# Order of VectorE's split-offs, place of a transpose step, two weight forms and a drain in a two-layer decoder trunk

## The chip, the cores and the metric

The kernel runs on 1 core of one Trainium2 chip. The metric is the device time of one execution in microseconds; 3 executions are shown for the kernel before. The engines are TensorE (PE in the profile; PEld is its weight load), VectorE (DVE), ScalarE (ACT), GpSimd (POOL) and SyncE (SP), each with its own in-order queue of instructions; transfers are issued from SP's and POOL's queues.

## The reference

Two decoder layers on one sequence of 256 tokens with 1024 features, all in float32. Each layer adds to h an attention (16 heads of 64), a gated feed-forward part of width 2816 and a gated input embedding. Layer 0's attention has a learned forget gate added to the logits, layer 1's a relative-position bias; with 256 tokens there is a single block of keys, so both are plain causal attentions with a bias.

```python
for i in range(DEPTH):
    u = _rmsnorm(h, attn_norm_g[i])
    ...
    h = h + _merge_heads(o) @ fox_w_o[j]
    ...
    u = _rmsnorm(h, ffn_norm_g[i])
    gu = u @ ffn_w_in[i]
    h = h + (jax.nn.silu(gu[..., :D_FF]) * gu[..., D_FF:]) @ ffn_w_out[i]
    gate = jax.nn.sigmoid(_rmsnorm(h, ple_norm_g[i]) @ ple_w_gate[i])
    h = h + gate * (p[i] @ ple_w_up[i])
return _rmsnorm(h, final_norm_g)
```

## The kernel before

**Three matmuls for one.** Each float32 operand is split into a high half (rounded to fp32r) and a low half (what is left), and `mm3` makes high by high, high by low and low by high.

**The weights' path.** All weights are one stream of 512 KB tiles in the order of use. SP loads tile i into `raw` (6 buffers; line 153, for the gapped form line 178, for the entry form line 138). ScalarE copies it to `whi` (line 157), VectorE subtracts to get `wlo` (line 158); both have 6 buffers. So the load of raw i + 6 is issued when wlo i is made, and whi i + 6 waits until PE has used whi i. Each matmul triple reads whi twice and wlo once, and the third matmul of a step in the program's order is the first that needs wlo. The triples of two or four heads or tiles may be interleaved.

**Forms.** `blocks()` gives eight blocks of 128 columns side by side; with ENTRY the first two blocks' wlo lie 8 columns further on and the rest 64 (two subtractions, of 256 and 768 columns, line 142). `gapped()` leaves a gap behind the first block in whi and wlo alike (1080 columns, line 180); the host packs its weights with that gap.

**Attention.** `_plan` gives the steps of a layer: `qk` j is `project(j)`, which makes pair j's q and k (pq, 48 matmuls out of two weights) and calls `scale()`: VectorE multiplies by the norm's row (qkt, line 453), ScalarE makes qkh (line 273) and VectorE qkl (line 274). `scores` of two pairs runs the matmuls sp out of qkt, qkh and qkl, then VectorE adds the bias (e, eight instructions, line 484), ScalarE takes the exponential with a sum (line 488), VectorE the reciprocal (rc, line 497). For pairs 0 to 5 ScalarE applies it (line 506), VectorE transposes (et, line 512) and GpSimd sends it through DRAM and loads it back (back). For pairs 6 and 7 VectorE applies it itself (line 501), and the step `turn` transposes on PE (pp, line 531), with ScalarE evicting into pt (line 534). `values` of two pairs makes po out of back or pt and v, and splits it into o's high half (ScalarE, line 273) and low half (VectorE, line 274). `wo` (hf, c) multiplies o of pairs 2c and 2c + 1 by one weight tile, 24 matmuls into two banks. The banks of wo (four) stay open over the layer; the other steps turn over the rest of the eight banks.

**What sets the order.** The tile framework's scheduler orders each engine's instructions by the order in the code and by priorities; `tc.issue_after(x)` adds an edge from x to what is made inside. Weights are made well ahead of their use, as buffers allow.

The plan's part around the change, and the split before it:

```python
("values", 0, 1), ("scores", 4, 5), ("wo", 0, 0), *pairs(6),
("values", 2, 3), ("scores", 6, 7), ("wo", 1, 0), ("wo", 0, 1), ("wo", 1, 1),
("values", 4, 5), ("turn", 6, 7), ("wo", 0, 2), ("values", 6, 7), ("wo", 1, 2)]
```

Of the kernel before, what the change touches and what calls it, by code (L numbers as in the profile page):

```python
# [30 lines left out]
ALU = mybir.AluOpType  # L31
# [43 lines left out]
def trunk(ctx: ExitStack, tc: tile.TileContext, xh, xg, wx, xr, pt, w, cst, gf, rel, hot, rvm, out):  # L75
# [10 lines left out]
    def f32(ap):  # L86
        return ap.bitcast(F32)
# [37 lines left out]
    hr = hw[:, 2].rearrange("p (k s) -> p k s", s=S)  # L125
    hx = [gx[:, GX - S:], hw[:, 0, 0:S], hw[:, 1, 0:S]] + [hr[:, k] for k in range(KT - 3)]

    def half(at=0, entry=0):


        i = state["next"]
        state["next"] += 1
        if i not in (1, 2):
            raw = work.tile([P, HW + LINE], F32, tag="raw", bufs=RAW, name=f"raw{i}")
        ht, lt = (work.tile([P, HW + 2 * LINE], F32R, tag=n, bufs=6, name=f"{n}{i}") for n in ("whi", "wlo"))
        hi, lo = ht[:, at:at + HW], lt[:, at:at + HW]
        if entry:
            state["sp"] = nc.sync.dma_start(raw[:, 0:HW], w[i - 2][:, 0:HW])
            nc.scalar.activation(hi, raw[:, 0:HW], AF.Copy)  # L139
            ats = [(at + FURTHER, 0, entry), (at + LINE, entry, HW)]  # L140
            for a, c0, c1 in ats:
                nc.vector.tensor_tensor(lt[:, a + c0:a + c1], raw[:, c0:c1], f32(hi[:, c0:c1]), op=ALU.subtract)  # L142
            return hi, [lt[:, a + k * P:a + (k + 1) * P] for a, c0, c1 in ats for k in range(c0 // P, c1 // P)]
        if i in (1, 2):
            raw = hw[:, i - 1, S:]
        parts = 2 if i < 2 else 1
        for q in range(parts):
            c = slice(q * HW // parts, (q + 1) * HW // parts)
            if i in (1, 2):
                at = slice(c.start + (S if q else 0), c.stop + S)  # L150
                nc.sync.dma_start(hw[:, i - 1, at], wx[i - 1][:, at])
            else:
                state["sp"] = nc.sync.dma_start(raw[:, c], w[max(i - 2, 0)][:, c])
            if i + q == 0:
                nc.vector.tensor_copy(hi[:, c], raw[:, c])
            else:
                nc.scalar.activation(hi[:, c], raw[:, c], AF.Copy)  # L157
            nc.vector.tensor_tensor(lo[:, c], raw[:, c], f32(hi[:, c]), op=ALU.subtract)  # L158
        return hi, lo

    def later(to, src):
# [9 lines left out]
    def gapped(first=0):  # L171

        i = state["next"]
        state["next"] += 1
        raw = work.tile([P, HW + LINE], F32, tag="raw", bufs=RAW, name=f"raw{i}")
        at = slice(APART + FURTHER, APART + FURTHER + WW)
        ht, lt = (work.tile([P, HW + 2 * LINE], F32R, tag=n, bufs=6, name=f"{n}{i}")[:, at] for n in ("whi", "wlo"))
        state["sp"] = nc.sync.dma_start(raw[:, 0:WW], w[i - 2])
        nc.scalar.activation(ht, raw[:, 0:WW], AF.Copy)
        nc.vector.tensor_tensor(lt, raw[:, 0:WW], f32(ht), op=ALU.subtract)  # L180
        cs = [bool(n) * GAP + n * P for n in (_entered(first).index(k) for k in range(KT))]
        return [[t[:, c:c + P] for c in cs] for t in (ht, lt)]

# [87 lines left out]

    def split(hi, lo, src):
        nc.scalar.activation(hi, src, AF.Copy)  # L273
        nc.vector.tensor_tensor(lo, src, f32(hi), op=ALU.subtract)

    def tokens(o, x, t, w, start, stop):

# [115 lines left out]
    def attention(layer, nm, mid, early, nf):  # L393
# [26 lines left out]

        o = work.tile([P, NP, 2, S], F32R, tag="act", name=f"o{layer}")
        oh, ol = o[:, :, 0], o[:, :, 1]
        qk, pq, sm, pts = {}, {}, {}, {}
        bias = add = None

        def project(j):

            bk = bank(f"pq{layer}_{j}")
            for a in range(2):
                if layer and j == 2 and a == 0:  # L430
                    hi, lo = gapped()
                else:
                    hi, lo = blocks(ENTRY if j == 0 and a == 0 else ())
                for k in range(KT):
                    last = mm3(bk[:, a * S:(a + 1) * S], (hi[k], lo[k]), nm.k(k),
                               start=(k == 0), stop=(k == KT - 1))
                if (j, a) == (layer, 0):
                    with tc.issue_after(last.ins), tc.high_priority():
                        nm.spread(-0.125)
                        scale()  # L440
                if layer and j == 0 and a == 0:
                    with tc.issue_after(last.ins):
                        nm.root()
            pq[j] = bk
            if (j, layer) != (0, 1):
                scale()

        def scale():

            for j in sorted(pq):  # L450
                bk = pq.pop(j)
                t = work.tile([P, 2, S], F32, tag="qkt", bufs=2, name=f"qkt{layer}_{j}")
                nc.vector.tensor_tensor(t.rearrange("p a s -> p (a s)"), bk,
                                        nm.row.rearrange("p a s -> p (a s)"), op=ALU.mult)

                th = work.tile([P, 3 * P], F32R, tag="qkh", bufs=2, name=f"qkh{layer}_{j}")
                tl = work.tile([P, 3 * P], F32R, tag="qkl", bufs=2, name=f"qkl{layer}_{j}")
                split(th, tl, t.rearrange("p a s -> p (a s)")[:, P:])
                qk[j] = t, th, tl

        def scores(*js):

            rows = [slice(s * DH, (s + 1) * DH) for s in range(2)]
            heads = [(2 * j + s, d, qk[j], bank(f"sp{layer}_{2 * j + s}")) for j in js for s, d in enumerate(rows)]
            for _, d, (t, _, _), sp in heads:
                mm(sp[:, 0:P], t[d, 0, 0:P], t[d, 1, 0:P], start=True, stop=add is None, skip_group_check=True)
            for n, (q, k) in enumerate(((1, 1), (1, 2), (2, 1))):
                for _, d, t, sp in heads:
                    got = mm(sp[:, P:3 * P], t[q][d, 0:P], t[k][d, P:], start=False, stop=(n == 2 and add is None),
                             skip_group_check=True)  # L470
            if add:
                for i, _, _, sp in heads:
                    got = add(i, sp)
            sl = (slice(0, P), slice(P, 3 * P))
            es = []
            for n, j in enumerate(js):
                del qk[j]
                e = work.tile([P, 2, 3 * P], F32, tag="e", bufs=4, name=f"e{layer}_{j}")
                mn = tiny.tile([P, 2, 2, 2], F32, tag="mn", bufs=4, name=f"mn{layer}_{j}")
                es.append((j, e, mn))  # L480
                for s in range(2):
                    i, _, _, sp = heads[2 * n + s]
                    for q, b in enumerate(bias(i)):
                        last = nc.vector.tensor_tensor_reduce(e[:, s, sl[q]], sp[:, sl[q]], b, 1.0, 3.0e38,
                                                              ALU.add, ALU.min, mn[:, 0, s, q:q + 1])
                for s in range(2):
                    for q in range(2):
                        nc.scalar.activation(e[:, s, sl[q]], e[:, s, sl[q]], AF.Exp, scale=-1.0,  # L488
                                             bias=mn[:, 0, s, q:q + 1], accum_out=mn[:, 1, s, q:q + 1])
            with tc.issue_after(last.ins):  # L490
                for j, e, mn in es:
                    finish(j, e, mn, sl)
# [262 lines left out]
    def ple(nm, ut):  # L755
# [19 lines left out]
        for c in range(4):  # L775
            pair_unit(bks[0], c, half(), nm.k)
            if c == 1:
                nm.root()
                table(AF.Sigmoid, nm.col[:, 0:1])
            if c == 2:  # L780
                for hf in range(2):
                    for t in range(2):
                        turn(t, hf)
# [85 lines left out]
def _plan(layer):  # L869

    def pairs(j):
        return [("qk", j), ("qk", j + 1)]

    first = ([("row", k) for k in range(4)] + [("gate",)] if layer == 0 else
             [("v", 0, 0), ("v", 0, 1), ("v", 1, 0), ("v", 1, 1), ("root",)])
    return [*first, ("qk", 0), ("bias",), ("qk", 1),
            ("v", 0, 2), ("v", 0, 3), ("scores", 0, 1), *pairs(2),
            ("v", 1, 2), ("scores", 2, 3), ("v", 1, 3), *pairs(4),
            ("values", 0, 1), ("scores", 4, 5), ("wo", 0, 0), *pairs(6),
            ("values", 2, 3), ("scores", 6, 7), ("wo", 1, 0), ("wo", 0, 1), ("wo", 1, 1),  # L880
            ("values", 4, 5), ("turn", 6, 7), ("wo", 0, 2), ("values", 6, 7), ("wo", 1, 2)]


def _entered(first):
# [130 lines left out]
```

## Time and profile before

| what | value |
|---|---|
| median of 3 executions | 652.67 us (651.58 to 658.07) |
| profiled execution, its own time | 652.5 us |
| its span | 650.7 us |
| mean granted TensorE clock | 0.996 |
| matmuls on PE | 5320, busy 638.6 us |
| VectorE, ScalarE, GpSimd busy | 449.6, 381.8, 46.8 us |

The span runs from the first to the last instruction, and the profiled execution's own time is 1.8 us longer. A row of the timeline gives the start, the busy time, the engine, the line, the operation with the tile written and those read, the count, and in brackets the idle time before it with what ended it. The windows view gives for a stretch its length, PE's busy time with the count of matmuls, the granted clock, the share of the DMA engines and GB/s. A waits row reads: who waited, for whom, us in total, times, longest.

### The profile page before, as it was taken

How to read it: one execution, taken by the hardware profiler on the slowest of the kernel's cores; microseconds unless marked ns; L12 is line 12 of the kernel's file. 1: busy time of each engine (PE TensorE's matmuls, PEld its weight loads, DVE VectorE, ACT ScalarE, POOL GpSimd, SP SyncE). 2: the span in 40 equal slices, each digit the busy share in tenths (PEclk: the TensorE clock that was granted, in tenths of full speed). 3: DMA queues.
4: the chain of work that ended last, by engine and by line, in shares of the span. 5: the costliest groups of instructions: out<-in, count | busy, mean ns of one | idle time of the engine just before them, and what ended most of it. 6: DMA issues, size and time to landing. Idle time of an engine off the chain costs nothing.

```text
span 650.7 us, 13215 instructions
## 1 busy us (share of the span) xinstructions
PE 638.6 (98%) x5320; PEld 614.9 (94%) x5320; DVE 449.6 (69%) x730; ACT 381.8 (59%) x662; POOL 46.8 (7%) x81
## 2 busy tenths in 40 slices
PE   9999999999999999999999999999999999999994
PEld 7998998999999999999989999899999999999984
DVE  6877794786666666658696877578666666666764
ACT  7788764664444444456766887657444444444762
POOL 1003330100000000000000333000000000000001
PEclk9999999999999999999999999999999999999998
DMA  8859884397676666666467688635766666666401
GB/s 337 301 182 311 255 261 134 103 316 235 193 234 207 232 201 210 194 191 195 162 241 278 203 264 264 179 121 182 234 190 193 194 191 194 195 212 192 159 1 66
DMA packets 39582, 133.51 MB, mean 205 GB/s; under 512 B 4896, under 2 KB 8032, under 8 KB 39520
## 3 DMA queue, kind: packets, MB, share of 16 engines
q1 hardware_dynamic: 35840, 122.81, 59.2%
q0 software_dynamic: 3264, 9.44, 4.6%
q8 instruction: 42, 0.69, 0.4%
q10 hardware_dynamic: 416, 0.40, 0.2%
q14 instruction: 20, 0.16, 0.1%
HBM read 126.84 MB, written 8.94 MB: 209 GB/s over the span
## 4 chain that ended last, share of the span: by engine, by line
PE 86%; ACT 5%; issue 4%; DVE 4%; DMA 1%; POOL 0%; POOLq 0%; ACTq 0%
PE gu L92 37%; PE fo L92 18%; PE pq L92 9%; PE wo L92 7%; PE v L92 5%; PE pg L92 5%; DVE wlo L158 2%; PE pu L92 2%; ACT e L488 2%; ACT whi L157 1%; PE po L92 1%; ACT e L506 1%; PE sp L92 1%; DMA gx<-xg 1%; ACT v L419 1%
## 5 line engine op out<-in xcount | busy, mean ns | idle before, releaser
L158 DVE TENSOR_TENSOR wlo<-raw,whi 128x1024 fp32r<-128x1024 f32 (+1 forms) x192 | 232.3, 1217 | 101.6 <-ACT whi L157 101.2
L157 ACT ACTIVATE whi<-raw 128x1024 fp32r<-128x1024 f32 (+1 forms) x191 | 199.1, 1054 | 139.9 <-issue 55.9
L92 PE MATMUL gu<-g,whi 128*128 128x256 f32 x1408 | 241.9, 277 | 0.0
L92 PEld LDWEIGHTS gu<-g,whi 128*128 128x128 f32 x1408 | 212.4, 188 | 0.0
L92 PE MATMUL gu<-g,wlo 128*128 128x256 f32 x704 | 194.7, 277 | 0.0
L92 PEld LDWEIGHTS gu<-g,wlo 128*128 128x128 f32 x704 | 132.2, 188 | 0.0
L92 PE MATMUL fo<-fp,whi 128*128 128x256 f32 x704 | 121.1, 276 | 0.0
L92 PEld LDWEIGHTS fo<-fp,whi 128*128 128x128 f32 x704 | 106.3, 188 | 0.1
L92 PE MATMUL fo<-fp,wlo 128*128 128x256 f32 x352 | 97.3, 276 | 0.0
L92 PE MATMUL pq<-g,whi 128*128 128x256 f32 x512 | 90.0, 280 | 0.0
L92 PEld LDWEIGHTS pq<-g,whi 128*128 128x128 f32 x512 | 78.3, 189 | 0.6 <-issue 0.2
L92 PE MATMUL pq<-g,wlo 128*128 128x256 f32 x256 | 71.4, 279 | 0.0
L92 PEld LDWEIGHTS fo<-fp,wlo 128*128 128x128 f32 x352 | 66.1, 188 | 0.0
L92 PEld LDWEIGHTS pq<-g,wlo 128*128 128x128 f32 x256 | 48.1, 188 | 0.0
L273 ACT ACTIVATE fp<-sg 128x256 fp32r<-128x256 f32 x44 | 18.2, 417 | 49.3 <-DVE sg L657 49.3
L92 PE MATMUL wo<-o,whi 128*128 128x256 f32 x256 | 45.5, 281 | 0.0
L229 POOL TENSOR_TENSOR col<-ms,nhalf 128x2 f32<-128x2 f32 x6 | 9.4, 1564 | 473.7 <-DVE ms L227 473.7
L142 DVE TENSOR_TENSOR wlo<-raw,whi 128x256 fp32r<-128x256 f32 (+1 forms) x40 | 26.0, 688 | 24.2 <-ACT whi L139 24.2
L92 PE MATMUL v<-whi,g 128*128 128x512 f32 x128 | 40.8, 394 | 0.4 <-ACT g L195 0.4
L92 PEld LDWEIGHTS wo<-o,whi 128*128 128x128 f32 x256 | 38.7, 188 | 1.1 <-issue 0.6
L653 DVE TENSOR_TENSOR gut<-gu,row 128x512 f32<-128x512 f32 x44 | 30.0, 690 | 10.4 <-PE gu L92 10.3
L139 ACT ACTIVATE whi<-raw 128x1024 fp32r<-128x1024 f32 x20 | 21.2, 1062 | 26.7 <-PE gu L92 24.0
(159 smaller groups left out, 771.1 us busy)
## 6 DMA issues: line engine op xcount, KB each, us to landing
raw<-w SPq DMA_DIRECT2D x210, 512.0 KB, 4.2
d<-et POOLq DMA_DIRECT2D x12, 384.0 KB, 3.5
back<-d POOLq DMA_DIRECT2D x48, 96.0 KB, 6.9
d<-d SPq DMA_DIRECT2D x4, 768.0 KB, 5.6
bias<-d SPq DMA_DIRECT2D x4, 512.0 KB, 6.4
raw<-w SPq DMA_DIRECT2D x3, 540.0 KB, 3.5
h<-xh SPq DMA_DIRECT2D x4, 256.0 KB, 7.3
hw<-wx SPq DMA_DIRECT2D x1, 640.0 KB, 6.4
```

What stands on the lines that cost most here:

```text
L92: state["pe"] = nc.tensor.matmul(*a, **k)
L139: nc.scalar.activation(hi, raw[:, 0:HW], AF.Copy)
L142: nc.vector.tensor_tensor(lt[:, a + c0:a + c1], raw[:, c0:c1], f32(hi[:, c0:c1]), op=ALU.subtract)
L157: nc.scalar.activation(hi[:, c], raw[:, c], AF.Copy)
L158: nc.vector.tensor_tensor(lo[:, c], raw[:, c], f32(hi[:, c]), op=ALU.subtract)
L229: nc.gpsimd.tensor_tensor(self.col, ms, nhalf, op=ALU.pow)
L273: nc.scalar.activation(hi, src, AF.Copy)
L419: nc.scalar.activation(v[:, t, hf * HC:(hf + 1) * HC], bks[t], AF.Copy, scale=nm.col[:, t:t + 1])
L488: nc.scalar.activation(e[:, s, sl[q]], e[:, s, sl[q]], AF.Exp, scale=-1.0, bias=mn[:, 0, s, q:q + 1], accum_out=mn[:, 1, s, q:q + 1])
L506: nc.scalar.activation(e[:, s, sl[q]], e[:, s, sl[q]], AF.Copy, scale=rc[:, s, q:q + 1])
L653: nc.vector.tensor_tensor(t.rearrange("p a s -> p (a s)"), bks[f], nm.row.rearrange("p a s -> p (a s)"), op=ALU.mult)
```

## The change

It has four parts.

- A new function `behind` makes an instruction with an edge from `state["dv"]`. `scores` sets that to the low half (qkl) of its last pair. Every wlo made after the first `scores` goes through `behind`, so it may not be issued ahead of that qkl.
- In the plan `("turn", 6, 7)` stands ahead of `("values", 4, 5)`.
- The first half of qk 4 has the entry form in both layers, and layer 1's first half of qk 2 is no longer gapped; the host's packing follows.
- GpSimd drains behind the call of the last norm's `root`.

```diff
+    def behind(make):
+
+        if "dv" not in state:
+            return make()
+        with tc.issue_after(state["dv"].ins):
+            return make()
...
-                nc.vector.tensor_tensor(lt[:, a + c0:a + c1], raw[:, c0:c1], f32(hi[:, c0:c1]), op=ALU.subtract)
+                behind(lambda: nc.vector.tensor_tensor(lt[:, a + c0:a + c1], raw[:, c0:c1], f32(hi[:, c0:c1]),
+                                                       op=ALU.subtract))
...
-            nc.vector.tensor_tensor(lo[:, c], raw[:, c], f32(hi[:, c]), op=ALU.subtract)
+            behind(lambda: nc.vector.tensor_tensor(lo[:, c], raw[:, c], f32(hi[:, c]), op=ALU.subtract))
...
-        nc.vector.tensor_tensor(lo, src, f32(hi), op=ALU.subtract)
+        return nc.vector.tensor_tensor(lo, src, f32(hi), op=ALU.subtract)
...
-                if layer and j == 2 and a == 0:
-                    hi, lo = gapped()
-                else:
-                    hi, lo = blocks(ENTRY if j == 0 and a == 0 else ())
+                hi, lo = blocks(ENTRY if j in (0, 4) and a == 0 else ())
...
-                split(th, tl, t.rearrange("p a s -> p (a s)")[:, P:])
+                low[j] = split(th, tl, t.rearrange("p a s -> p (a s)")[:, P:])
...
+            state["dv"] = low[js[-1]]
...
                 nm.root()
+                nc.gpsimd.drain()
...
-            ("values", 4, 5), ("turn", 6, 7), ("wo", 0, 2), ("values", 6, 7), ("wo", 1, 2)]
+            ("turn", 6, 7), ("values", 4, 5), ("wo", 0, 2), ("values", 6, 7), ("wo", 1, 2)]
```

What that does to the queues, in layer 1. In the names below the number behind a weight's whi or wlo is its place in the stream (133, 134 and 135 belong to the three wo steps behind `scores` 6, 7, and 136 to wo (0, 2)); o1 is o of layer 1, and the numbers behind the last underscore only tell tiles apart.

VectorE between the last projection of layer 1 and the first e of its last scores, before:

```order
L453 TENSOR_TENSOR qkt1_7_5118<-pq1_7_5057,row3_4344 128x512
L158 TENSOR_TENSOR wlo138_5392<-raw138_5390,whi138_5391 128x1024
L274 TENSOR_TENSOR qkl1_7_5121<-qkt1_7_5118,qkh1_7_5120 128x384
L274 TENSOR_TENSOR o1_4160<-po1_2_5124,o1_4160 128x256
L274 TENSOR_TENSOR o1_4160<-po1_3_5125,o1_4160 128x256
L484 ISA e1_6_5158,mn1_6_5159<-sp1_12_5138,bias1_4199 128x128
```

and with the change:

```order
L458 TENSOR_TENSOR qkt1_7_5120<-pq1_7_5059,row3_4345 128x512
L282 TENSOR_TENSOR qkl1_7_5123<-qkt1_7_5120,qkh1_7_5122 128x384
L282 TENSOR_TENSOR o1_4161<-po1_2_5126,o1_4161 128x256
L282 TENSOR_TENSOR o1_4161<-po1_3_5127,o1_4161 128x256
L166 TENSOR_TENSOR wlo133_5192<-raw133_5190,whi133_5191 128x1024
L490 ISA e1_6_5160,mn1_6_5161<-sp1_12_5140,bias1_4200 128x128
```

Before, wlo138 stands between qkt and qkl of pair 7; with the change qkl and both o come first, and wlo133, which had been made long before, stands behind them.

VectorE behind the e's of those scores, before:

```order
L497 RECIPROCAL rc1_6_5178<-mn1_6_5159 128x4
L501 TENSOR_TENSOR e1_6_5158<-e1_6_5158,rc1_6_5178 128x2x128
L501 TENSOR_TENSOR e1_6_5158<-e1_6_5158,rc1_6_5178 128x2x256
L497 RECIPROCAL rc1_7_5182<-mn1_7_5169 128x4
L501 TENSOR_TENSOR e1_7_5168<-e1_7_5168,rc1_7_5182 128x2x128
L501 TENSOR_TENSOR e1_7_5168<-e1_7_5168,rc1_7_5182 128x2x256
L158 TENSOR_TENSOR wlo139_5432<-raw139_5430,whi139_5431 128x1024
L158 TENSOR_TENSOR wlo140_5487<-raw140_5485,whi140_5486 128x1024
L158 TENSOR_TENSOR wlo141_5493<-raw141_5491,whi141_5492 128x1024
```

and with the change:

```order
L503 RECIPROCAL rc1_6_5180<-mn1_6_5161 128x4
L166 TENSOR_TENSOR wlo134_5222<-raw134_5220,whi134_5221 128x1024
L507 TENSOR_TENSOR e1_6_5160<-e1_6_5160,rc1_6_5180 128x2x128
L507 TENSOR_TENSOR e1_6_5160<-e1_6_5160,rc1_6_5180 128x2x256
L503 RECIPROCAL rc1_7_5184<-mn1_7_5171 128x4
L166 TENSOR_TENSOR wlo135_5252<-raw135_5250,whi135_5251 128x1024
L507 TENSOR_TENSOR e1_7_5170<-e1_7_5170,rc1_7_5184 128x2x128
L507 TENSOR_TENSOR e1_7_5170<-e1_7_5170,rc1_7_5184 128x2x256
L166 TENSOR_TENSOR wlo136_5320<-raw136_5318,whi136_5319 128x1024
L166 TENSOR_TENSOR wlo137_5364<-raw137_5362,whi137_5363 128x1024
L166 TENSOR_TENSOR wlo138_5394<-raw138_5392,whi138_5393 128x1024
L166 TENSOR_TENSOR wlo139_5434<-raw139_5432,whi139_5433 128x1024
```

Before, no wlo of the wo steps is left to make here, and o of pairs 4 and 5 follows wlo141; with the change wlo134 to wlo138 stand between and behind the reciprocals and products, and o of pairs 4 and 5 follows wlo140.

ScalarE behind the last exponentials of layer 1, before:

```order
L157 ACTIVATE whi139_5431<-raw139_5430 128x1024
L157 ACTIVATE whi140_5486<-raw140_5485 128x1024
L157 ACTIVATE whi141_5492<-raw141_5491 128x1024
L273 ACTIVATE o1_4160<-po1_4_5278 128x256
L273 ACTIVATE o1_4160<-po1_5_5279 128x256
L534 ACTIVATE pt1_12_5296<-pp1_12_5292 128x384
L534 ACTIVATE pt1_13_5302<-pp1_13_5298 128x384
L534 ACTIVATE pt1_14_5308<-pp1_14_5304 128x384
L534 ACTIVATE pt1_15_5314<-pp1_15_5310 128x384
```

and with the change:

```order
L165 ACTIVATE whi139_5433<-raw139_5432 128x1024
L165 ACTIVATE whi140_5488<-raw140_5487 128x1024
L165 ACTIVATE whi141_5494<-raw141_5493 128x1024
L540 ACTIVATE pt1_12_5284<-pp1_12_5280 128x384
L540 ACTIVATE pt1_13_5290<-pp1_13_5286 128x384
L540 ACTIVATE pt1_14_5296<-pp1_14_5292 128x384
L540 ACTIVATE pt1_15_5302<-pp1_15_5298 128x384
L281 ACTIVATE o1_4161<-po1_4_5304 128x256
L281 ACTIVATE o1_4161<-po1_5_5305 128x256
```

The evictions of the transposes (pt) now stand ahead of those of po (o), and directly behind whi141. On PE the order moves in the same way: pp ahead of po, and po directly ahead of wo (0, 2).

GpSimd's drain comes, in the program as built, near the start of its queue, behind the fill of the tile `zero`; the rest of its queue is the same.

More of the change, by code (lines that the diff above doesn't have):

```diff
@@ L179, in gapped @@
         nc.scalar.activation(ht, raw[:, 0:WW], AF.Copy)
-        nc.vector.tensor_tensor(lt, raw[:, 0:WW], f32(ht), op=ALU.subtract)
+        behind(lambda: nc.vector.tensor_tensor(lt, raw[:, 0:WW], f32(ht), op=ALU.subtract))
         cs = [bool(n) * GAP + n * P for n in (_entered(first).index(k) for k in range(KT))]
@@ L422, in attention @@
         oh, ol = o[:, :, 0], o[:, :, 1]
-        qk, pq, sm, pts = {}, {}, {}, {}
+        qk, pq, low, sm, pts = {}, {}, {}, {}, {}
         bias = add = None
@@ L963 @@
                 j = n[0]
-                seq += [_gapped(a[2 * j]) if j == 2 and i else a[2 * j], a[2 * j + 1]]
+                seq += a[2 * j:2 * j + 2]
         seq += [_wide(wo, NP - 2, hf) for hf in range(2)]
```

## The prediction

> **What bounds the kernel now.** I read the page first: one core, span 650.7 us in an execution of 652.5 us, 0.2 us under the median of 652.67. All sums below are made against the 652.5; on the median's scale they stand 0.2 higher.
>
> ```profile
> span 650.7 us, 13215 instructions
> PE 638.6 (98%) x5320; PEld 614.9 (94%) x5320; DVE 449.6 (69%) x730; ACT 381.8 (59%) x662; POOL 46.8 (7%) x81
> ...
> PE 86%; ACT 5%; issue 4%; DVE 4%; DMA 1%; POOL 0%; POOLq 0%; ACTq 0%
> ```
>
> TensorE (PE) is busy for 98% of the span and carries 86% of the chain that ended last. So a gain can come from two places only: gaps of PE, or matmuls that go faster. The windows view (us, PE busy and count, granted clock, DMA share, GB/s) shows that the feed-forward part has no gaps at all:
>
> ```profile
> 136.00:291.00 155.00, 155.00 (x1367) 1.00 0.69 218
> ```
>
> The gaps stand in the two attention layers. The waits of PE's weight loads, and of SP's queue, name them:
>
> ```profile
> PEld sp L92 <- DVE qkl L274: 3.0, 6, 0.7
> ...
> SPq L153 <- DVE wlo L158: 281.8, 120, 9.9
> ```
>
> The scores wait for the low half of q and k, six times, 3.0 us in all. The second row matters for what the change gives back: SP issues the load of a weight's raw tile when VectorE has made the wlo of the weight six places earlier (six raw buffers), so a late wlo makes a late load.
>
> **Part 1, the two forms.** The windows of the projections, 96 matmuls each (24 in the third):
>
> ```profile
> 39.85:50.84 10.99, 10.99 (x96) 1.00 0.55 212
> 58.74:70.14 11.40, 11.40 (x96) 1.00 0.92 307
> 336.39:339.14 2.75, 2.75 (x24) 1.00 1.08 397
> 355.34:366.76 11.42, 11.42 (x96) 1.00 0.39 143
> 373.81:385.21 11.40, 11.40 (x96) 1.00 0.83 258
> 76.71:87.68 10.97, 10.97 (x96) 1.00 0.75 252
> ```
>
> At one granted clock the same 96 matmuls take 10.99 or 11.40 us, so there are two paces, 114.5 and 118.8 ns per matmul. The slow ones are qk4, 5 (behind a v step) and layer 1's qk2, 3 (the gapped form behind scores); plain blocks behind scores (39.85; 76.71 behind wo) and the entry form behind v (336.39, 2.75 per 24) are quick. The change gives qk4 the entry form and qk2 the plain one, so each slow block takes the quick pace: -0.41, -0.41, -0.43, together **-1.25**. From below it could be nothing, if the pace hangs on something else, for instance on where the stage begins; from above 1.25 is all. I take the whole, since every block in those two places and forms went quick. The longer raw load of the gapped form falls away unseen, behind SP's waits.
>
> [...]
>
> **Part 2, the wlo's put behind qkl.** The sp matmuls in eight windows, four of layer 0 and four of layer 1:
>
> ```profile
> 38.14:39.85 1.71, 1.71 (x24) 1.00 0.79 218
> 53.68:55.89 2.21, 1.97 (x24) 1.00 1.06 303
> 71.59:73.87 2.28, 1.97 (x24) 1.00 1.02 269
> 89.13:91.41 2.28, 1.96 (x24) 1.00 0.97 252
> 353.99:355.34 1.35, 1.35 (x20) 1.00 0.48 79
> 369.60:370.96 1.36, 1.36 (x20) 1.00 1.00 330
> 386.66:388.75 2.09, 1.61 (x20) 1.00 0.97 288
> 404.02:405.96 1.94, 1.62 (x20) 1.00 1.09 293
> ```
>
> A stage that does not wait takes 1.71 us in layer 0 and 1.35 in layer 1. The excess of the others is 0.50 + 0.57 + 0.57 + 0.74 + 0.59 = 2.97 us: the most that this part can win. It wins it only if the wlo that steps back isn't itself waited for. That is read from the timeline around the last scores of layer 1 (pq7 ends at 402.57, called T1 below; columns: start, us):
>
> ```profile
> 402.57 1.06 ACT L157 ACTIVATE whi<-raw 128x1024 fp32r<-128x1024 f32 x1 [1.56 <-PE pq L92]
> 403.53 0.51 ACT L273 ACTIVATE qkh<-qkt 128x384 fp32r<-128x384 f32 x1
> ...
> 403.66 1.22 DVE L158 TENSOR_TENSOR wlo<-raw,whi 128x1024 fp32r<-128x1024 f32 x1 [0.28 <-ACT whi L157]
> 404.80 0.55 DVE L274 TENSOR_TENSOR qkl<-qkt,qkh 128x384 fp32r<-128x384 f32 x1
> 405.27 0.74 DVE L274 TENSOR_TENSOR o<-po,o 128x256 fp32r<-128x256 f32 x2
> 405.94 0.29 DVE L484 CUSTOM_DVE_ANT_0 e<-sp,bias 128x128 f32<-128x128 f32 x1
> ...
> 408.23 0.18 DVE L497 RECIPROCAL rc<-mn 128x4 f32<-128x4 f32 x1
> 408.44 1.03 DVE L501 TENSOR_TENSOR e<-e,rc 128x256 f32<-128x256 f32 x2
> ...
> 411.15 1.22 DVE L158 TENSOR_TENSOR wlo<-raw,whi 128x1024 fp32r<-128x1024 f32 x1
> ```
>
> Before, the wlo of 403.66 stands ahead of qkl and costs it 1.14 us. It belongs to the weight of the wo step that comes directly behind the scores. Put behind qkl and the o pair (as the order now has it), it starts at about T1 + 2.8 and ends at T1 + 4.0. wo needs it in its third matmul, which came at 405.96 + 0.25 - 402.57 = T1 + 3.64. So the scores' gain of 0.59 turns into a wait of wo that ends 0.4 later than before. The same count from the end of pq5 (T0) gives wo's third matmul at T0 + 4.15 in both layers. Before, it came 0.34 behind the scores' ends of 73.87 and 388.75, with pq5's ends at 70.14 and 385.21: T0 + 4.07 and 3.89. So +0.08 and +0.26. Only the scores of pairs 2, 3 in layer 0, behind which projections with weights made long ago follow, keep their 0.50. That is the first term: **-0.50**.
>
> The new order has more in it. In layer 1 not one but all later wlo's fall behind the eight e's (2.29 us from 405.94 to 408.23) and the first reciprocal, which waits for four exps of ScalarE. After T0 the e's end at T0 + 6.3, the reciprocal runs at 6.5, and the next wlo (the first of pair 6's projection) ends at 7.7, where PE wants it at 6.88 (4.15, 22 matmuls of wo more, 0.23). With the 0.26 above, pq7 ends **+1.1** later. In layer 0 two wlo's precede the e's, and the third (e's to 7.5, wlo 1.22) is ready at T0 + 8.9, where PE wants it 24 projection matmuls (2.75) later than in layer 1, at 9.6: no loss.
>
> After T1 come three wo steps. Layer 1: the first waits until T1 + 4.0, ends at 6.5; the second wants its wlo at 6.75, which comes at 7.7, so this stretch ends 1.3 late, at T1 + 13.05. Layer 0 has two wlo's ahead of the e's again and ends at most 0.1 late.
>
> **Part 3, the turn ahead of values 4, 5.** Here the old order shows what covered what (layer 1):
>
> ```profile
> 414.33 1.52 PE L92 MATMUL po<-back,v 128*64 128x256 f32 x16
> 415.79 0.87 PE L531 MATMUL pp<-con,e 128*128 128x128 f32 x6
> 416.91 0.87 PE L531 MATMUL pp<-con,e 128*128 128x128 f32 x6 [0.25 <-ACT pt L534]
> ...
> 414.38 1.06 ACT L157 ACTIVATE whi<-raw 128x1024 fp32r<-128x1024 f32 x1 [1.66 <-PE wo L92]
> 415.68 0.66 ACT L273 ACTIVATE o<-po 128x256 fp32r<-128x256 f32 x2 [0.25 <-PE po L92]
> 416.37 0.87 ACT L534 ACTIVATE pt<-pp 128x384 f32<-128x384 f32 x2
> ...
> raw<-w SPq DMA_DIRECT2D x210, 512.0 KB, 4.2
> ...
> 417.54:420.40 2.86, 2.86 (x24) 1.00 0.61 188
> 103.00:105.91 2.91, 2.91 (x24) 1.00 0.55 179
> ```
>
> po's eviction into o (high and low) ran while PE did the transposes; wo(0,2) then started at 417.54 with o ready. Now the transposes come first and wo(0,2) stands right behind po. Besides, po's banks are those of the first two pp tiles, which ScalarE empties (pt, 0.44 each) behind a whi whose raw tile is the one issued by the third wlo after T1. In layer 1 that wlo ends at T1 + 10.05; with 4.2 for the load and 0.1 for the issue the raw lands at 14.35, whi ends at 15.4, the two pt at 16.25, po's 16 matmuls at 16.9, the other two pt at 17.1, o's high halves from there to 17.75, its low half at 17.95. wo(0,2) needs that low half in its third matmul: T1 + 18.0, against 417.54 + 0.35 - 402.57 = 15.3. **+2.7**, the 1.3 of the stretch before included. In layer 0 the third wlo ends at T1 + 8.9, the pt's end at 16.0 and o's high half at 16.65, but VectorE is then busy without a gap (eight e's, two reciprocals, two times 1.03 of line 501 and eight wlo's at 1.14) until 16.7, and o's low half comes at 17.05. Before, wo(0,2) of layer 0 had its third matmul at T1 + 15.65 (start 103.00, pq7 end 87.68): **+1.4**, and with the 0.08 of T0 **+1.5**. Both these terms hold what part 2 cost after T1.
>
> **Part 4, the drain.** In the program as built GpSimd's drain has no work ahead of it but a few memsets. Where the source puts it, it costs nothing either: GpSimd idles there for 14.53 us, and 0.2 us of wait would hide in it.
>
> ```profile
> 640.44 0.19 POOL L816 TENSOR_TENSOR colf<-ssf,msf 128x1 f32<-128x1 f32 x1 [14.53 <-issue]
> ```
>
> **The sum.** Layer 0: -0.50 - 0.41 + 1.5 = +0.6. Layer 1: -0.43 - 0.41 + 1.1 + 2.7 = +3.0. Together +3.6: 652.5 + 3.6 = 656.1, on the median's scale 656.3. I give **656.3**.
>
> **The rivals.**
> - *All the waits go* (not slower). The wlo's are in time after all, because the e's and wlo's interleave better than I count, and pp's wait for pt (0.25 in the row of 416.91; 0.5 for both layers) goes too: -2.97 - 1.25 - 0.5 = -4.7, 648.0 on the median's scale. For it: the 3.0 us of the waits' row are real. Against it: the displaced wlo is needed 0.4 us before it can be ready. It decides if that wlo ends before T1 + 3.4 and the whi ahead of the pt's before T1 + 13. Chance 0.14 (646.5 to 650).
> - *They cancel.* The stretch after T1 loses only about half, for instance because the raw behind the third wlo lands 1 us earlier and ScalarE takes the pt's first: +0.5 to +1.5 for the turn instead of +4.2 in all; 652.6 to 653.6. Chance 0.16.
> - *Loads come late* (slower by over 1%). The loads behind the late wlo's are issued closer to their use and share their engines with the loads of back on GpSimd's queue, whose median is 6.9 us. If the deciding raw takes 6.9 instead of 4.2, wo(0,2) moves by 2.7 more in layer 1 and by up to 2.4 in layer 0 (where VectorE hides 0.4): 656.3 + 5.1 = 661.4. It decides from a landing of 5.8 us on. Chance 0.12.
>
> ```profile
> back<-d POOLq DMA_DIRECT2D x48, 96.0 KB, 6.9
> ```
>
> - *The forms do nothing* (the change there doesn't do what it says): the sum without its first part, 657.5. [...] For it speaks that blocks of one place and form were seen one to three times only. Chance 0.1.
>
> **How the numbers follow.** My forecast has 0.48 and runs from 654 to 658; the forms' rival lies beside it up to 659. The range of 8 in 10 leaves out most of the first rival and the end of the third: 650 to 660. About 1% (6.5 us) is what a measurement of this kernel can tell from no change. Faster by over 1% needs more than every named gap: 0.01. Slower by over 1% (from 659.2) is the late loads with a tail of the forecast: 0.12. The rest, 0.87, is within 1%.
>
> **What would show it.** Right: sp of all stages at 1.71 and 1.35 with no wait for qkl; wo behind the scores waits for wlo; layer 1's first matmuls of pair 6 wait 0.8 us for wlo; wo(0,2) starts with a wait for o of 1.5 us and more; 96 projection matmuls in 11.0 us everywhere; feed-forward windows without gaps as before. Wrong: no wait of PE for wlo in wo, po directly behind pp without a wait for ScalarE's pt, or a projection that stays at 11.4.

## The result

| | before | with the change |
|---|---|---|
| median of 20 executions each | 653.25 us (651.58 to 665.32) | 656.88 us (655.21 to 668.52) |
| profiled execution: own time, span | 652.5, 650.7 us | 658.88, 656.6 us |
| ratio | | 1.0057, 95% interval 1.0031 to 1.0082 |

The change makes the kernel 0.6% slower. Its profiled execution is 2.0 us above its median, so the difference of the two profiles (5.9 us of span) is larger than that of the medians (3.6 us). Single executions of either kernel fall into groups some 6 us apart, by the pace that each feed-forward part happens to take (last section); both profiles belong to their lowest group, where the medians are 652.67 (12 of 20) and 656.44 (15 of 20). The ratios leave out executions over 1.5% above the fastest of their own kernel, so that they come out too high where none fell into the lowest group. Below, kernels are therefore also compared by the lengths of their two attention stretches in the profile.

The windows view gives a profile in four stretches: layer 0's attention (from the first matmul of its forget gate to the first feed-forward one), layer 0's feed-forward part, and the same two of layer 1 (its attention from the first matmul of v). Before:

```profile
16.54:115.94 99.40, 98.28 (x831) 1.00 0.75 240
115.94:302.38 186.44, 186.44 (x1643) 1.00 0.67 210
325.48:430.49 105.01, 103.96 (x838) 1.00 0.72 232
430.49:617.35 186.86, 186.86 (x1619) 1.00 0.62 191
```

With the change:

```profile
16.96:117.39 100.43, 98.36 (x832) 1.00 0.72 234
117.39:303.82 186.43, 186.43 (x1642) 1.00 0.66 210
326.93:436.37 109.44, 106.11 (x839) 0.98 0.67 222
436.37:623.22 186.85, 186.85 (x1618) 1.00 0.62 191
```

The feed-forward parts are equal to 0.01 us. The attention grew by 1.03 us in layer 0 and 4.43 in layer 1. The rest of the 5.9 is 0.4 us of start ahead of the first stretch. What PE waits for now, by the waits view:

```profile
PE wo L92 <- DVE wlo L166: 2.0, 4, 0.7
PE po L92 <- ACT pt L540: 1.1, 2, 0.7
PE sp L92 <- ACT qkh L281: 1.1, 2, 0.8
...
PE wo L92 <- ACT o L281: 0.5, 2, 0.3
PE pq L92 <- DVE wlo L166: 0.4, 1, 0.4
```

The wait of the scores for qkl is gone. Five others stand in its place, four of them named beforehand (wlo in wo and in pq, pt ahead of po, o ahead of wo); the scores' wait for qkh is new. The scores' windows with the change (columns as before) show where it sits, in the last row of each layer:

```profile
54.01:55.71 1.70, 1.70 (x24) 1.00 0.65 162
71.03:72.74 1.71, 1.71 (x24) 1.00 0.68 193
88.53:91.16 2.63, 2.23 (x24) 1.00 0.28 72
387.29:388.65 1.36, 1.36 (x20) 1.00 0.61 167
405.96:408.71 2.75, 1.88 (x20) 1.00 0.66 180
```

ScalarE's timeline in layer 0 tells why (pq7 ends at 87.08): the whi that stands ahead of qkh waits 1.99 us for its load.

```profile
85.08 1.07 ACT L165 ACTIVATE whi<-raw 128x1024 fp32r<-128x1024 f32 x1 [0.43 <-DMA raw<-w]
88.14 1.06 ACT L165 ACTIVATE whi<-raw 128x1024 fp32r<-128x1024 f32 x1 [1.99 <-DMA raw<-w]
89.11 0.51 ACT L281 ACTIVATE qkh<-qkt 128x384 fp32r<-128x384 f32 x1
```

The three loads of that time were issued when VectorE had made three wlo's behind the e's of pairs 4 and 5 (76.87 to 80.4 us). Before, the same wlo's, of weights 22 to 24, lay ahead of those scores (66.68 to 70.6 us). The last of the three loads is that of weight 30, whose whi stands ahead of qkh. SP's issue of it and its time to landing, before and with the change:

```profile
70.66 0.33 SPq L153 DMA_DIRECT2D raw<-w  x1
raw<-w SPq DMA_DIRECT2D x1, 512.0 KB, 8.8
...
80.46 0.33 SPq L161 DMA_DIRECT2D raw<-w  x1
raw<-w SPq DMA_DIRECT2D x1, 512.0 KB, 7.6
```

Before, it was issued 17.0 us ahead of the end of pq7 (87.68), so that 8.8 us did no harm; with the change it was issued 6.6 us ahead and landed 1.0 late. In layer 1 the same holds of weight 138: issued 16.6 us ahead before and 5.9 with the change, where it took 7.4 us. So a wlo that steps back is paid twice: by its own user, and six weights later by whoever stands behind the whi of the late load.

### The profile page after: what moved, and what is told of

Read it like the earlier page. It is cut to its first block, busy times and chain, and to the rows that moved or that the text cites. A ratio compares the mean times of both kernels' runs of the same rounds, so it can differ in the third digit from the quotient of the medians.

```text
span 656.6 us, 13188 instructions
## 1 busy us (share of the span) xinstructions
PE 641.6 (98%) x5320; PEld 617.4 (94%) x5320; DVE 448.4 (68%) x732; ACT 381.6 (58%) x662; POOL 46.9 (7%) x81
## 4 chain that ended last, share of the span: by engine, by line
PE 87%; DVE 5%; issue 3%; ACT 2%; DMA 2%; POOL 0%; POOLq 0%; DVEq 0%; ACTq 0%; SPq 0%
PE gu L92 37%; PE fo L92 18%; PE pq L92 12%; PE v L92 7%; PE pg L92 5%; PE wo L92 4%; DVE wlo L166 3%; DMA raw<-w 2%; PE pu L92 2%; PE sp L92 1%; PE po L92 1%; ACT whi L165 1%; PE cold L92 1%; DVE e L490 1%; ACT e L494 1%
## 5 line engine op out<-in xcount | busy, mean ns | idle before, releaser
L166 DVE TENSOR_TENSOR wlo<-raw,whi 128x1024 fp32r<-128x1024 f32 (+1 forms) x191 | 229.7, 1215 | 86.7 <-ACT whi L165 86.4
L92 PE MATMUL fo<-fp,wlo 128*128 128x256 f32 x352 | 97.3, 276 | 0.0
L92 PE MATMUL wo<-o,whi 128*128 128x256 f32 x256 | 47.4, 287 | 0.6 <-ACT o L281 0.5
L149 DVE TENSOR_TENSOR wlo<-raw,whi 128x256 fp32r<-128x256 f32 (+1 forms) x44 | 28.6, 687 | 24.5 <-ACT whi L146 24.5
L146 ACT ACTIVATE whi<-raw 128x1024 fp32r<-128x1024 f32 x22 | 23.3, 1061 | 27.1 <-PE gu L92 27.1
L92 PE MATMUL wo<-o,wlo 128*128 128x256 f32 x128 | 36.6, 288 | 2.0 <-DVE wlo L166 2.0
```

Source lines behind the costliest of these rows:

```text
L92: state["pe"] = nc.tensor.matmul(*a, **k)
L149: behind(lambda: nc.vector.tensor_tensor(lt[:, a + c0:a + c1], raw[:, c0:c1], f32(hi[:, c0:c1]), op=ALU.subtract))
L166: behind(lambda: nc.vector.tensor_tensor(lo[:, c], raw[:, c], f32(hi[:, c]), op=ALU.subtract))
```

## The experiments

The theory: each edge holds back not only the wlo that collided with qkl, but all that come later in the code, weights whose users are near included, and with them the loads six places on. The turn then costs something of its own, and the forms win 1.2 us. The rivals: the turn carries the loss; the forms bring nothing; the drain costs something. "Attention" in the tables is the sum of the two attention stretches in the profile: 204.4 us before the change, 209.9 with it. Single blocks in these stretches also take one of two paces (96 matmuls of a projection in 11.0 or 11.4 us, 72 of wo in 8.3 to 8.7) in places where no edit aimed at it, so that a sum is good to about half a microsecond. The medians of the kernel before are those measured alongside.

### One part at a time

For the edges alone, the plan, the forms and the drain were set back to those of before. For the turn alone and the forms alone this line was left out, so that no wlo gets an edge:

```diff
-            state["dv"] = low[js[-1]]
```

> Only the edges of the wlo's behind qkl; the plan, the forms and GpSimd's queue are those of before. Theory (the loss comes from holding back every later wlo, and with it the loads six places on): 4 to 5 us slower than before (657 to 658), scores of pairs 6, 7 at 2.6 us or more in both layers with a wait for ScalarE's qkh, wo behind the scores waits for wlo. Rival (the loss comes from the turn ahead of the values): within 1 us of before, at 652 to 654, since the scores win what wo loses.

> Only the turn of pairs 6, 7 ahead of values 4, 5. Theory (it exposes the split of po in front of wo(0,2), but ScalarE's whi ahead of the evictions is in time here): 0.8 to 1.9 us slower, 654 to 655, of it 0.3 to 1.0 in each layer between the end of the three wo steps and the first low-half matmul of wo(0,2). Rival 1 (the turn carries the loss): 3 us slower or more. Rival 2 (it removes the wait of pp for pt, 0.5 us in both layers, and costs nothing): 0.5 us faster.

> Only the two q halves in other forms (entry form for qk 4, plain for layer 1's qk 2). Theory (a block of projections takes one of two paces, and these two forms at these places take the quick one): 1.2 us faster, about 652.0 for 653.2; the windows of qk 4, 5 in both layers and of layer 1's qk 2, 3 at 11.0 us instead of 11.4. Rival (the pace hung on when the stage began, not on the form): those windows stay at 11.4 and the time within 0.3 us of before.

| only | median (before) | ratio, interval | attention | against before |
|---|---|---|---|---|
| the edges | 664.69 (659.44) | 1.0128 (1.0057 to 1.0198) | 209.4 | +5.0 |
| the turn | 660.39 (659.44) | 1.0009 (0.9969 to 1.005) | 205.4 | +1.0 |
| the forms | 659.45 (659.44) | 1.0047 (1.0006 to 1.0088) | 204.4 | 0.0 |

The edges carry the loss; the rival with the turn falls. Executions of the same group say the same: in the middle one of the three the medians are 663.73 us for the edges, 659.96 for the turn and 659.18 for the forms, against 659.35 before. The edges' waits alone are those of the whole change, with pp in po's place behind pt:

```profile
PE wo L92 <- DVE wlo L166: 2.1, 5, 0.7
PE pp L540 <- ACT pt L543: 1.8, 2, 1.0
PE sp L92 <- ACT qkh L281: 1.2, 1, 1.2
...
PE pq L92 <- DVE wlo L166: 0.5, 1, 0.5
```

Only in layer 1 did the scores of pairs 6, 7 wait for qkh; in layer 0 they took 1.71 us, so half of that expectation missed. The turn costs 1.0 us, inside what was expected; 0.5 of it in each layer lies between the third wo step and the end of wo (0, 2). The forms gave a surprise: their three projection windows did go from 11.4 to 11.0 us, and yet nothing was left of it. The scores of pairs 4, 5 took 1.0 us of the 1.2 back (2.28 to 2.54 us in layer 0, 2.09 to 2.82 in layer 1):

```profile
70.82:73.36 2.54, 2.00 (x24) 1.00 1.02 295
...
392.38:395.20 2.82, 2.00 (x20) 1.00 0.89 283
```

A projection that ends earlier finds VectorE still at the same wlo's. The interval above 1 for the forms I do not read as a loss, since the profile's stretches and the middle groups are equal.

### Holding fewer wlo's

If holding all of them is the fault, holding only the one that stood between qkt and qkl should win. In `narrow` the edge goes to five weights only, with the forms of the change, the plan of before and no drain:

```diff
-        if "dv" not in state:
+        at = (19, 25, 30, 133, 138)
+        if state["next"] - 1 not in at:
             return make()
-        with tc.issue_after(state["dv"].ins):
+        with tc.issue_after(state["dv"][state["next"] - 1].ins):
             return make()
...
-            state["dv"] = low[js[-1]]
+            state.setdefault("dv", {})
+            for i in {(0, 2): (19,), (0, 4): (25,), (0, 6): (30,), (1, 4): (133,), (1, 6): (138,)}.get((layer, js[0]), ()):
+                state["dv"][i] = low[js[-1]]
```

> The forms of the change, the plan of before, and the edge behind qkl for five wlo's only: those which stood between qkt and qkl of the last pair before the waiting scores (weights 19, 25 and 30 in layer 0, 133 and 138 in layer 1), each five places ahead of its use. Theory (the edge is good where the wlo has time, and the loss comes from holding the others): scores at 1.7 us in layer 0 and 1.4 in layer 1, no wait of wo or pq for wlo, 3 to 4.2 us faster than before, 649 to 650. Rival (late loads follow even from one wlo, or the scores then wait for qkh): at most 1.5 us faster.

658.73 against 659.44 us, ratio 0.9976 (0.9928 to 1.0024); attention 203.7, 0.7 less than before. No wait for wlo, late load or qkh, as the theory has it, but far less gain than it claimed (0.4 us of what is missing is the pace of qk 6, 7 in layer 0, 11.40 us for 10.97). The scores of pairs 4, 5 had become worse:

```profile
70.69:73.91 3.22, 2.35 (x24) 1.00 0.93 280
...
392.33:394.70 2.37, 2.00 (x20) 1.00 0.93 256
```

VectorE's timeline in layer 0 shows it: pq5 ended at 69.24, but qkt started at 71.14, behind two wlo's.

```profile
68.86 2.35 DVE L167 TENSOR_TENSOR wlo<-raw,whi 128x1024 fp32r<-128x1024 f32 x2
71.14 0.68 DVE L459 TENSOR_TENSOR qkt<-pq,row 128x512 f32<-128x512 f32 x1
```

So the wlo ahead of qkt has to step back too. `narrow2` also holds weights 24 and 132; `narrow3` in addition 18, 23 and 29:

```diff
-        at = (19, 25, 30, 133, 138)
+        at = (18, 19, 23, 24, 25, 29, 30, 132, 133, 138)
...
-            for i in {(0, 2): (19,), (0, 4): (25,), (0, 6): (30,), (1, 4): (133,), (1, 6): (138,)}.get((layer, js[0]), ()):
+            for i in {(0, 2): (18, 19), (0, 4): (23, 24, 25), (0, 6): (29, 30), (1, 4): (132, 133), (1, 6): (138,)}.get((layer, js[0]), ()):
```

> As narrow, with two more wlo's held: of weights 24 and 132, which stood ahead of qkt of pair 5. Theory (with quick projections VectorE comes late to qkt because two wlo's in a row stand ahead of it, so that the forms' gain came back as a wait of the scores of pairs 4, 5): these scores go from 3.2 us in layer 0 and 2.4 in layer 1 to at most 1.8 and 1.5, and the two attention stretches together are 3.5 to 4.5 us shorter than before the change. Rival (the scores then wait for ScalarE's qkh, which stands behind a whi): they stay above 2.2 us and the stretches within 1.5 us of before.

> As narrow2, with weights 18, 23 and 29 of layer 0 held as well, so that no wlo stands directly ahead of qkt of the second pair. Theory (what is left of the scores' waits in layer 0 is VectorE's wlo ahead of qkt): scores of pairs 2, 3 and 4, 5 and 6, 7 of layer 0 at 1.7 us, where narrow2 had 1.8, 2.1 and 2.3, and layer 0's attention stretch 0.8 to 1.1 us shorter than narrow2's. Rival (from three wlo's on the loads come late, as in the change): wo or the scores behind them wait for wlo or qkh, and the stretch is no shorter or longer.

| | median (before) | ratio, interval | lowest group (before's) | attention | against before |
|---|---|---|---|---|---|
| narrow2 | 656.56 (658.39) | 0.9960 (0.9913 to 1.0007) | 650.36 (652.77) | 202.0 | -2.4 |
| narrow3 | 655.18 (658.94) | 0.9956 (0.9911 to 1.0000) | 648.58 (652.79) | 200.7 | -3.7 |

`narrow2` won less than expected (qk 6, 7 of layer 0 took 11.40 us here too): in layer 1 the scores of pairs 4, 5 are free (1.36 us), in layer 0 they still took 2.09, and those of pairs 6, 7 took 2.30. `narrow3` mends that. All its scores in layer 0 take 1.71 us, and no more than pp's 0.5 us for pt is left of the attention's waits:

```profile
53.56:55.27 1.71, 1.71 (x24) 1.00 1.00 294
70.59:72.30 1.71, 1.71 (x24) 1.00 0.87 237
87.57:89.28 1.71, 1.71 (x24) 1.00 1.09 347
...
383.71:385.07 1.36, 1.36 (x20) 1.00 0.91 267
400.34:401.88 1.54, 1.54 (x20) 1.00 1.08 301
```

Its layer 0 stretch is 97.3 us (narrow2: 98.9, more of a gain than the 0.8 to 1.1 expected; 0.4 of it is the pace of qk 6, 7). Its lowest group lies 4.2 us below that of before, its second 3.9 (655.28 against 659.21). By its attention and its lowest group it is the fastest kernel of this study; the interval over all groups just reaches 1.

### What the forms are worth

`narrow3` with the two q halves set back to the forms of before:

> As narrow3, with the two q halves in the forms of before. Theory (the quick forms are worth 1.2 us, but only where VectorE has qkt and qkl ready when the shorter projection ends; in the run with the forms alone the scores' wait gave it back): the two attention stretches together are 1.0 to 1.3 us longer than narrow3's, all of it in the three projection windows (11.4 for 11.0 us), with the scores at 1.7 and 1.4 us. Rival (the forms bring nothing in any case): within 0.4 us of narrow3.

650.14 us against 658.87 before, ratio 0.9932 (0.9888 to 0.9976); attention 201.6, 0.9 more than narrow3 and so just under the 1.0 to 1.3 expected. The three windows are back at 11.4 (+1.2), and a wo block in layer 1 took the quick pace this time (-0.3). So the forms are worth their 1.2 us in those windows once VectorE is in time. (The ratio is better than narrow3's only because 7 of its 12 executions were in the lowest group and 4 of narrow3's 12. Against the kernel before, measured alongside each, the lowest group is 2.6 us lower and the second 3.5, where narrow3 has 4.2 and 3.9: 1.6 and 0.5 us for the forms.)

### The late load, the turn and the drain

In `qkh_first`, the change without the drain, ScalarE's whi of weights 30 and 138 gets an edge behind qkh of pair 7:

```diff
+            elif i in (30, 138):
+                with tc.issue_after(state["hi"].ins):
+                    nc.scalar.activation(hi[:, c], raw[:, c], AF.Copy)
             else:
                 nc.scalar.activation(hi[:, c], raw[:, c], AF.Copy)
...
+            if js[0] == 6:
+                state["hi"] = high[7]
```

> The change without the drain, and ScalarE's whi of weights 30 and 138 put behind qkh of pair 7 (it stood ahead of it). Theory (the scores of pairs 6, 7 wait because that whi waits for a load that a late wlo has delayed): these scores go from 2.6 and 2.7 us to 1.7 and 1.4; the wo steps behind them still wait for wlo, and the attention stretches together are 1 to 2.3 us shorter than the change's. Rival (qkh is late for another reason, the load on ScalarE): the scores stay above 2.2 us.

In its single execution (664.34 us) the scores of pairs 6, 7 take 1.71 and 1.36 us, so it was that whi that held them up. Attention is 209.0, 0.9 less than the change's first profile and 1.0 less than the change without the drain, just at the lower bound of what was expected. Against the first profile layer 1 fell by 2.4 to 107.1 us and layer 0 rose by 1.5 to 101.9: there po now waits 2.72 us for pt, whose whi is late in turn, and behind that wait the TensorE clock fell to a half:

```profile
102.82 2.83 PE L92 MATMUL po<-back,v 128*64 128x256 f32 x16 [2.72 <-ACT pt L546]
...
102.20:105.61 3.41, 2.79 (x16) 0.50 1.00 356
```

Those 16 matmuls take 1.52 us in the change's profiles, so that 1.3 of the 1.5 us are the clock. The delay moves on; it is not gone.

> The edges and the forms, with the plan of before (values 4, 5 ahead of the turn) and no drain. Theory (the turn costs its own 1 us, added to what the edges cost): about 1 us less than the change in the two attention stretches together, most of it between the third wo step and wo(0,2). Rival (behind late wlo's the turn fills a wait that is there anyway): no less than the change.

> The change without GpSimd's drain; everything else is the same. Theory (the drain has nothing to wait for): the time of the change, the stretch from its matmul stage pf to the feed-forward part within 1.5 us of the change's in each layer, and the scores of pairs 6, 7 again longer than before the change. Rival (the drain costs time on GpSimd in front of the attention's loads): 0.5 us faster or more, by a shorter start.

> The change once more, for a second profile of it. Theory (its profiled execution was a long one, since late loads land at varying times): the wait of the scores of pairs 6, 7 and of the evictions behind the delayed loads differ by up to 1.5 us from the first profile, and the two attention stretches together are 3.5 to 6 us longer than before the change. Rival (the profile was typical): within 0.3 us of the first profile in each of those stages.

| | median (before) | ratio, interval | attention |
|---|---|---|---|
| edges and forms, no turn | 659.36 (658.39) | 1.0046 (0.9991 to 1.0101) | 207.4 |
| the change without the drain | 663.05 (658.39), 4 runs | 1.0124 (1.0055 to 1.0194) | 210.0 |
| the change once more | 663.49 (658.94) | 1.0058 (1.0007 to 1.011) | 208.6 |

The change once more is 1.3 us shorter in attention than in its first profile, and the stages differ as expected of late loads: the scores of pairs 6, 7 took 1.71 and 1.81 us (2.63 and 2.75 in the first). Without the turn the attention is 2.5 us shorter than in the first profile of the change, 1.2 than in the second, and 2.6 than in the run without the drain, which differs from it by the turn alone. In the part that the turn touches, from the end of the third wo step to the end of wo (0, 2), the difference is 0.9, 2.5 and 2.5 us. So among late loads the turn can cost more than the 1.0 it costs by itself, where "about 1 us" was expected: po then waits for a pt behind a late whi (2.8 us in the second profile and without the drain, 1.1 in the first), where without the turn pp waits 1.1 us for it. Without the drain the attention is not shorter; its medians rest on four executions, none of them in the lowest group, and are no evidence against it.

### The pace of the feed-forward part

`ffn_entry` is narrow2 with the one gapped weight of each feed-forward part in the entry form (the host's packing follows):

```diff
-                if fs[0] == 2 and a:
-                    wt = gapped()
-                else:
-                    wt = blocks(ENTRY if fs[0] % 2 == 0 and a == 0 and fs[0] > 2 else ())
+                wt = blocks(ENTRY if fs[0] % 2 == 0 and a == (fs[0] == 2) else ())
```

> As narrow2, with the gapped weight behind the first break of each feed-forward part made in the entry form. Theory (the form of the first weight behind a break sets the pace of what follows, and the entry form always took the quick one in qk): every execution has both feed-forward parts at 186 to 187 us, and the times lie in one group near 650. Rival (the pace is set by something that varies between executions of one program): the feed-forward parts still take 186 or 193 us by chance, and the times lie in groups some 6 us apart.

The theory falls: 656.28 us (658.94 before; 0.9979, 0.9931 to 1.0026), with executions in all three groups, 1, 7 and 4 of them, and in its profile one part at 186.5 us and the other at 192.6.

## Why the prediction was right

The forecast was 656.3 us, the median 656.88; the sum of the terms was +3.6 us, and so is the difference of the medians. That they agree to 0.1 us is luck in part: executions of the same group differ by 3.8 us (lowest) and 4.2 (middle), and the attention by 5.5 us in the change's first profile and 4.2 in its second. By terms, against these two profiles:

- **Scores of pairs 2, 3, -0.50.** Measured 2.21 to 1.70, -0.51.
- **The forms, -1.25.** The windows of qk 4, 5 in both layers and of layer 1's qk 2, 3 went to 11.0 us, -1.22; so they did in all ten profiles with the new forms, and in all four with the old ones they took 11.4. The Trainium skill ("TensorE: Matmul & The Clock Gate", section "Back-to-back issue gap") says that in a stream of weight loads and matmuls the spacing is set by both; it states one rate for each of two widths. The two rates at one width in these windows (114.5 and 118.8 ns for 256 columns, at clock 1.00) it does not have. The experiments add the condition that the prediction did not see: by themselves these 1.2 us came back as a wait of the scores. They count here because the edges freed qkl.
- **wo behind scores 4, 5: +0.08 and +0.26.** Scores and wo together took 5.07 us for 5.12 in layer 0, and 5.15 for 4.94 in layer 1: -0.05 and +0.21. The scores' gain turned into wo's wait, as worked out, but the prediction gave the wlo the wrong owner. The one that stood ahead of qkl at 403.66 is of weight 138, five places ahead of its use; wo waits for that of weight 133, which had been made at 386.5 us before and which the edge moves to this place. The forecast took its times from the new order, where weight 133 does stand there, and so came out right. (The third matmul of wo came 0.33 us behind the scores, not 0.25, which moves T1 + 3.64 to 3.72 and makes the 0.4 a 0.3.) That the colliding wlo itself can step back at no cost is what `narrow` shows.
- **Pair 6's wait in layer 1, +1.1 with the 0.26.** pq of pairs 6, 7 took 12.07 and 12.15 us for 10.97, so T1 came 1.3 later in both. Not all of it is the wait. In the change without the drain the window waited as long for the same wlo and took 11.67 us, in `qkh_first` 11.74: 0.7 to 0.8 us is the wait, as counted (0.8). The other 0.4 is the slower pace, which these 96 matmuls took in the two profiles and which the sum did not have. Layer 0 lost nothing there (10.97), as predicted.
- **From T1 to the end of wo(0,2), +1.4 in layer 0 and +2.7 in layer 1.** The second profile has +1.4 and +3.2, the first +2.0 and +3.9. The chain held: wlo's behind the e's, the late raw, pt behind whi, then po, then o. Only the place of the wait was partly another: PE waits ahead of po for pt (1.1 us in the first profile, 2.8 in the second) and only 0.5 for o in both layers together, where 1.5 was named for each.

The 96 matmuls of pairs 6, 7 in layer 1, in the change's first profile and without the drain:

```profile
392.44:404.51 12.07, 11.66 (x96) 1.00 0.71 241
...
398.94:410.61 11.67, 11.27 (x96) 1.00 0.72 249
```

The step that was mis-sized is "qkl in time after T1": the prediction let the whi ahead of qkh start when pq7 ended, since it did so before. Its load is itself one of the delayed ones, issued some 6 us ahead of pq7's end where it had been 17, and it takes about as long as that: 7.6 us in layer 0 and 7.4 in layer 1 in the first profile, 5.5 and 6.5 in the second. In the first profile this put 0.9 us on the scores of layer 0 and 1.4 on those of layer 1, in the second 0 and 0.45. The rival *loads come late* was thus right in its mechanism and wrong in its place: the raw behind the third wlo, at which it looked, took 4.0 to 4.5 us in both profiles, about the 4.2 of the forecast. Why the loads of weights 30 and 138 take longer than the median of 4.2 us was not tested; they run beside GpSimd's transfers, and before the change they took 8.8 and 8.6 us unseen.

A further thing was not in the sum at all. In the first profile the TensorE clock fell in layer 1, behind the two waits of the scores and of wo:

```profile
406.40:409.80 3.40, 1.95 (x20) 0.97 0.70 186
409.80:413.10 3.30, 3.14 (x15) 0.51 0.54 168
```

The fall is at 409.6, in the last 0.2 us of the first row. For 3.3 us 15 matmuls ran where about 29 would have at the pace behind it; the three wo steps took 10.73 us in this profile and 9.86 in the second, where the clock stayed at 1.00. The difference of 0.87 is about this, less what the next wait for wlo would have taken anyway. The Trainium skill ("TensorE: Matmul & The Clock Gate", section "What's actually happening") says that the clock is halved after an idle window of about 3.4 us and that the window runs free. The trace agrees on the half and on the length, and differs on the idle: PE was busy for 1.95 of the 3.40 us before, and no single wait there was longer than 0.8 us. In the edges-only run two such waits in the same place left the clock at 1.00, in `qkh_first` it fell during the wait of 2.72 us. What decides between them stays open.

## What to carry to other kernels

An edge or a priority meant for one instruction should name that one. Put on all that come later in the code, it undoes the lead of everything that had been made ahead, and through a ring of buffers a late maker is also a late load. In a kernel that is 98% busy, a faster block is worth something only if what must be ready at its end comes from an engine with time to spare: the forms were worth 0 or 1.2 us depending on whether VectorE had qkt and qkl ready. And a step that has long been hiding an eviction (the transposes between po and wo) is doing work in its place, even when it waits a little itself.

## What the runs showed of the hardware that was not expected

The same program takes its feed-forward part at one of two paces. The rows are narrow3 (both parts quick) and the forms alone (both slow), with counts of matmuls equal to within one and the granted clock at 1.00:

```profile
113.81:300.25 186.44, 186.44 (x1643) 1.00 0.66 210
...
426.72:613.59 186.87, 186.87 (x1618) 1.00 0.62 191
```

```profile
115.53:308.81 193.28, 193.28 (x1643) 1.00 0.64 203
...
436.93:629.58 192.65, 192.65 (x1619) 1.00 0.59 185
```

That is 113.5 and 117.6 ns per matmul in layer 0, and 5.8 to 6.8 us a layer; executions of one kernel fall into three groups accordingly (652.79, 659.21 and 665.29 us for 13, 13 and 3 executions of the kernel before, measured together), and in the profiles of this study the group went with the number of slow parts, none, one or two. The pace was kept for a whole part, and the entry form did not set it. What sets it stays open: it was seen to differ between executions of the same program, and no experiment here steered it. Blocks of 96 matmuls show the same two paces. In qk 4, 5 and in layer 1's qk 2, 3 the form set it; yet qk 6, 7 of layer 0, whose form no run changed, took 10.97 us in nine profiles and 11.40 in five.
